# A new pair of heads every 8 hops of a two-way scan instead of every 13, and both chains of a pair in one tile

## The chip, the cores and the metric

The kernel runs on one core of one Trainium2 chip. The metric is the device time of one execution in microseconds (us). The core has five engines that the profile tells apart: PE (TensorE, the matrix products; its weight loads are listed as PEld), DVE (VectorE), ACT (ScalarE), POOL (GpSimd) and SP (SyncE, which here only issues DMAs). Each works through its own instructions in order and waits on semaphores for the others. Products are written to PSUM, everything else stands in SBUF, and large arrays in HBM.

## The reference

One layer of a model runs over 640 tokens: 512 latent tokens (group ii) and 128 context tokens (group i), with width 2048. After a wide input product, half of the channels go through a bidirectional delta-rule scan with 16 heads of 64 channels, the other half through a chunked gate (gMLP). Then come the output product, a SwiGLU block and the norms. The change touches the scan and what runs beside it:

```python
def _delta_scan(r, w, k, v, aa, bb, s0, reverse):
    def step(S, inp):
        r_t, w_t, k_t, v_t, a_t, b_t = inp
        sa = jnp.einsum('bhvk,bhk->bhv', S, a_t)
        S = S * w_t[:, :, None, :] + sa[..., None] * b_t[:, :, None, :] + v_t[..., None] * k_t[:, :, None, :]
        return S, jnp.einsum('bhvk,bhk->bhv', S, r_t)
    s_fin, ys = lax.scan(step, s0, xs, reverse=reverse)

def _rwkv7_bidir(p, s0, lp):
    ...
    for d in range(2):                      # forward, backward
        ...
        y, s_fin = _delta_scan(rh, decay, kd, vh, -kk, kk * heads(a), s0[:, d].astype(F32), reverse=(d == 1))
        out = out + _group_norm(y, lp['gn_w'], lp['gn_b']) + jnp.sum(rh * kd * lp['r_k'], axis=-1, keepdims=True) * vh
    o = (out.reshape(B, T, D_A) * gate).astype(dtype)

x = x + g1 * (jnp.concatenate([o_a, o_b], axis=-1) @ lp['w_out'])
```

The context scan starts from zero and its final states are an output; the latent scan starts from given states.

## The kernel before

The scan is done in chunks of 64 tokens: 8 chunks of the latents and 2 of the context. An earlier stage has written for each chunk and pair of heads a record to HBM (d_S: the matrices that carry a state over the chunk and that make its outputs), 128 partitions with 2 directions of 576 values, 576 KB. Eight pairs of heads (NPAIR) are worked through by the generator `recur(p)`. A pair has two chains: the latents with 8 steps, and the context with 2. A step takes three hops. In the first, PE multiplies the state by the record (w, L1464) and DVE adds what the record holds (W, L1469); the outputs of the step before are made here too (y, L1430 and L1435), and ACT takes them out with their sums (Y, L1449). In the second, PE makes u (L1480), and DVE and ACT copy the halves back into the record (L1483, L1484). In the third, PE makes the state's update (s, L1501) and DVE adds it to the decayed state (SG L1498, SN L1507; L1505 for a first step). A hop is one round of the loop at L1630; each generator in work goes one `yield` ahead per hop. `recur` starts and ends with a turn of the states (swap, L1406).

Three more things run in the same hops. `finish(p)` normalises the finished pair (POOL, ACT, DVE), turns it (pO, L1577), multiplies by the gate (pG, L1587) and stores it to d_o. A mixer, m3, hands out the second half of the output product: wide products of 128x320 (L1332 to L1334), which need pieces of w_out (raw, split into hi and lo), turned inputs (pxT, L1614) and add to x1T (L1345). `load_next` asks for the next record each time an output has been taken; there are 8 record buffers (NREC). SP issues all these loads in the order of its own list. PE's order in this stage is the order in which the program states the products; the other engines' orders and the places of the pools in SBUF are set by the framework when the program is built. The last products of the stage before (the gMLP's psp, with its additions sp on DVE) reach into the first hops.

OFF = 13 says how many hops lie between the starts of two pairs, so the loop has 13 x 7 + 26 = 117 hops, with two pairs in work. The names `ws`, `u`, `y0`, `y1`, `g` are PSUM tags: two buffers for `ws` (w, s and swap), one for each of the others.

## Time and profile before

| | |
|---|---|
| Time, median of 3 runs | 3182.96 us (3179.46 to 3184.34) |
| The profiled execution: its time | 3181.58 us |
| Its span, from first to last instruction | 3179.8 us |
| PE busy over the span | 3060.3 us (96%) |
| DVE busy over the span | 2321.0 us (73%) |
| First swap of the first pair | 1020.8 us from the span's start |
| Last swap of the last pair | 1307.7 us |

The views used below are the page, which sums up the whole span; the windows, which give each engine's busy time in a stretch, with the granted clock of PE, the mean busy share of the 16 DMA engines and what they moved; the waits, which say who waited for whom (total us, times, longest); the groups of instructions by line (busy time, mean ns of one, idle time of the engine just before them); the DMA issues; and the timeline, where a row is a start, a length, the engine, the line, output and inputs, and in brackets the engine's idle time before it and who ended it. A float32 product shows as two records there. Numbers such as 64*64 are the part of PE's array that the product takes. The ends of products are modelled, so starts are what is compared.

### The profile page before, as it was taken

The numbers are of one execution on the slowest core, as the hardware profiler recorded it, in microseconds if no ns is written. First come the engines' busy times: TensorE is split into PE (matmuls) and PEld (weight loads), VectorE is DVE, ScalarE is ACT, GpSimd is POOL, SyncE is SP. The second block draws the span as 40 slices with busy tenths as digits, with TensorE's granted clock in tenths as the row PEclk, the third lists the DMA queues.
The fourth block names the chain that finished last, engine by engine and source line by source line (L and its number), as shares of the span: only waits on it lengthen the run. The fifth ranks groups of instructions, "written<-read, shape, count | busy, mean of one in ns | idle before, by whom it ended". The sixth has DMA issues, their size and how long they took to land. (4 is left out here: it accounts for less than half of the span.)

```text
span 3179.8 us, 73098 instructions
## 1 busy us (share of the span) xinstructions
PE 3060.3 (96%) x28572; PEld 2860.0 (90%) x28572; DVE 2321.0 (73%) x4103; ACT 1449.0 (46%) x3173; POOL 1296.1 (41%) x1154
## 2 busy tenths in 40 slices
PE   7999999999998999999899999999999999999996
PEld 4788888888877777889899999999999999999996
DVE  4557686776756677677887787787877877877787
ACT  4244555555543443346444444444444444444365
POOL 1001222322321143320566566665666645554543
PEclk9999999999999999999999999999999999999998
DMA  9768988899886877455333443434334354554453
GB/s 342 241 187 240 237 236 213 214 233 235 223 228 190 251 240 246 134 153 174 105 119 118 127 123 107 124 116 126 120 108 130 107 183 146 163 163 141 115 174 122
DMA packets 742331, 552.97 MB, mean 174 GB/s; under 512 B 142112, under 2 KB 678720, under 8 KB 733152
## 3 DMA queue, kind: packets, MB, share of 16 engines
q1 hardware_dynamic: 727280, 529.73, 56.2%
q0 software_dynamic: 12288, 17.95, 2.4%
q8 instruction: 225, 3.69, 0.5%
q14 instruction: 122, 1.00, 0.1%
q10 hardware_dynamic: 2416, 0.60, 0.1%
HBM read 438.74 MB, written 111.69 MB: 173 GB/s over the span
## 5 line engine op out<-in xcount | busy, mean ns | idle before, releaser
L1932 PE MATMUL P<-xo,lo 128*128 128x320 f32 x2352 | 728.0, 310 | 7.5 <-DVE lo L1720 7.5
L1930 PE MATMUL P<-xo,hi 128*128 128x320 f32 x2352 | 728.1, 310 | 2.2 <-ACT hi L1719 2.2
L1931 PE MATMUL P<-xo,hi 128*128 128x320 f32 x2352 | 727.7, 309 | 0.0
L1720 DVE TENSOR_TENSOR lo<-raw,hi 128x512 fp32r<-128x512 f32 x532 | 506.0, 958 | 177.2 <-ACT hi L1719 175.4
L1719 ACT CAST hi<-raw 128x512 fp32r<-128x512 f32 x532 | 330.4, 622 | 505.5 <-PE P L1931 431.9
L1932 PEld LDWEIGHTS P<-xo,lo 128*128 128x128 f32 x2352 | 442.2, 188 | 8.0 <-DVE lo L1720 8.0
L1930 PEld LDWEIGHTS P<-xo,hi 128*128 128x128 f32 x2352 | 442.4, 188 | 2.4 <-ACT hi L1719 2.4
L1931 PEld LDWEIGHTS P<-xo,hi 128*128 128x128 f32 x2352 | 442.4, 188 | 0.0
L1830 POOL TENSOR_TENSOR raw<-raw 128x512 f32<-128x512 f32 x252 | 413.7, 1645 | 16.5 <-DVE lo L1720 3.3
L1930 PE MATMUL P<-xd,hi 128*128 128x320 f32 x1232 | 384.2, 312 | 8.5 <-ACT hi L1719 4.1
L106 PE MATMUL big<-h_hi,hi 128*128 128x320 f32 x1184 | 388.8, 328 | 0.7 <-DVE early L600 0.7
L1932 PE MATMUL P<-xd,lo 128*128 128x320 f32 x1232 | 384.3, 312 | 4.3 <-DVE lo L1720 4.0
L1931 PE MATMUL P<-xd,hi 128*128 128x320 f32 x1232 | 383.1, 311 | 0.0
L106 PE MATMUL big<-h_hi,lo 128*128 128x320 f32 x1184 | 365.5, 309 | 0.4 <-DVE lo L106 0.4
L106 PE MATMUL big<-h_lo,hi 128*128 128x320 f32 x1184 | 365.5, 309 | 0.0
L1830 POOL TENSOR_TENSOR t<-raw 128x512 f32<-128x512 f32 x84 | 134.8, 1605 | 460.6 <-DMA raw<-in_w_ffn_up_dram 399.2
L1719 ACT CAST hi<-rawd 128x512 fp32r<-128x512 f32 (+1 forms) x288 | 166.1, 586 | 230.0 <-PE P L1931 150.5
L106 PEld LDWEIGHTS big<-h_hi,hi 128*128 128x128 f32 x1184 | 223.7, 189 | 34.4 <-issue 29.0
L1720 DVE TENSOR_TENSOR lo<-rawd,hi 128x512 fp32r<-128x512 f32 (+1 forms) x288 | 217.5, 762 | 44.9 <-ACT hi L1719 41.5
L1930 PEld LDWEIGHTS P<-xd,hi 128*128 128x128 f32 x1232 | 233.4, 189 | 12.0 <-ACT P L2228 6.5
L1932 PEld LDWEIGHTS P<-xd,lo 128*128 128x128 f32 x1232 | 233.5, 190 | 7.1 <-DVE lo L1720 7.1
L1931 PEld LDWEIGHTS P<-xd,hi 128*128 128x128 f32 x1232 | 233.4, 189 | 0.0
(406 smaller groups left out, 6347.4 us busy)
## 6 DMA issues: line engine op xcount, KB each, us to landing
wt<-in_w_mod_dram SPq DMA_DIRECT2D x96, 1024.0 KB
raw<-in_w_ffn_gate_dram SPq DMA_DIRECT2D x182, 256.0 KB
raw<-in_w_ffn_up_dram SPq DMA_DIRECT2D x182, 256.0 KB
rec<-d_S SPq DMA_DIRECT2D x80, 576.0 KB
raw<-in_w_in_dram SPq DMA_DIRECT2D x166, 256.0 KB
rawd<-in_w_ffn_down_dram SPq DMA_DIRECT2D x128, 256.0 KB
raw<-in_w_out_dram SPq DMA_DIRECT2D x96, 256.0 KB
xd<-d_os SPq DMA_DIRECT2D x66, 320.0 KB
```

Source lines behind the costliest of these rows:

```text
L106: self.eng, self.run = eng, lambda: fn(*args, **kw)
L1719: S.copy(hi[:, 0:nk], raw[:, 0:nk])
L1720: V.tensor_sub(lo[:, 0:nk], raw[:, 0:nk], hi[:, 0:nk].bitcast(F32))
L1830: G.tensor_tensor(out=o[:, 0:nk], in0=p[:, 0:nk], in1=q[:, 0:nk], op=ALU.subtract)
L1930: TE.matmul(ps, hi[:, k, :], xk[:, 0, :], start=f, stop=False)
L1931: TE.matmul(ps, hi[:, k, :], xk[:, 1, :], start=False, stop=False)
L1932: TE.matmul(ps, lo[:, k, :], xk[:, 0, :], start=False, stop=l)
```

## The change

The distance of two pairs becomes 8 hops, so that three are in work in most hops, and the loop has 8 x 7 + 26 = 82. In a hop the pair in its second stage (u) now stands first, then the one in its first (w and y), then the one in its third (s). Both chains of a pair share one PSUM tile in each stage, and the products of both are stated before the first copy or addition. The tiles that a pair holds longer get more buffers: Y and ys five instead of three, ST/SN ten instead of seven, bv and g2r two instead of one. At the end of the loop the sixth pair is not finished yet, so its o block is loaded when it is.

```diff
 ROWO = 4
 RAWB = 13
 WTAIL = -12
-OFF = 13
+OFF = 8
 MB = 6
 KCOST = 35.0
 GORD = (0, 1, 1, 2, 2, 3, 3, 8)
...
             for d in range(2):
                 for h in range(2):
                     TE.matmul(ps[hsl(h), d, :], src[hsl(h), d, :], I2[hsl(h), :], start=True, stop=True)
-            o = sm.tile([P, 2, CH], F32, tag="ST", name="ST", bufs=7)
+            o = sm.tile([P, 2, CH], F32, tag="ST", name="ST", bufs=10)
             V.tensor_copy(o, ps)
             return o
 
         def recur(p):
 
             u = U[p]
-            u.Y = rw.tile([P, 2, NCH, CH], F32, tag=f"Y{p % 3}", name="Y")
-            u.ys = sm.tile([P, 2, NCH], F32, tag=f"ys{p % 3}", name="ys", bufs=1)
+            u.Y = rw.tile([P, 2, NCH, CH], F32, tag=f"Y{p % 5}", name="Y")
+            u.ys = sm.tile([P, 2, NCH], F32, tag=f"ys{p % 5}", name="ys", bufs=1)
             chains = [[False, swap(u.s0)], [True, None]]
             if p + 2 < NPAIR:
                 load_s0(p + 2)
...
 
             for step in range(len(LATC)):
                 act = [c for c in chains if step < len(seqs[c[0]])]
-                Ws = []
-                for ctx_, ST in act:
+                Ws = [None] * len(act)
+                if any(ST is not None for _, ST in act):
+                    ws = pws.tile([P, 2, 2, CH], F32, tag="ws", name="w_ps")
+                for e, (ctx_, ST) in enumerate(act):
                     r = recs[p, ctx_, step]
-                    if ST is None:
-                        Ws.append(None)
-                        continue
-                    w_ps = pws.tile([P, 2, CH], F32, tag="ws", name="w_ps")
-                    for d in range(2):
+                    if ST is not None:
+                        for d in range(2):
+                            for h in range(2):
+                                TE.matmul(ws[osl(h), e, d, :], r[hsl(h), d, F_R:F_R + CH], ST[hsl(h), d, :],
+                                          start=True, stop=True)
+                for e, (ctx_, ST) in enumerate(act):
+                    r = recs[p, ctx_, step]
+                    if ST is not None:
+                        W = Ws[e] = sm.tile([P, 2, CH], F32, tag="W", name="W", bufs=4)
                         for h in range(2):
-                            TE.matmul(w_ps[osl(h), d, :], r[hsl(h), d, F_R:F_R + CH], ST[hsl(h), d, :],
-                                      start=True, stop=True)
-                    W = sm.tile([P, 2, CH], F32, tag="W", name="W", bufs=4)
-                    for h in range(2):
-                        q = osl(h)
-                        V.tensor_add(W[q], w_ps[q], r[q, :, F_Z + CH * h:F_Z + CH * h + CH])
-                    Ws.append(W)
+                            q = osl(h)
+                            V.tensor_add(W[q], ws[q, e], r[q, :, F_Z + CH * h:F_Z + CH * h + CH])
                 outputs()
                 yield 1
                 both = pu.tile([P, 2, 2, CH], F32, tag="u", name="u_ps")
                 for e, ((ctx_, ST), W) in enumerate(zip(act, Ws)):
                     r = recs[p, ctx_, step]
-                    ups = both[:, e]
                     for d in range(2):
                         for h in range(2):
                             q = osl(h)
-                            TE.matmul(ups[q, d, :], r[q, d, F_T:F_T + CH],
+                            TE.matmul(both[q, e, d, :], r[q, d, F_T:F_T + CH],
                                       r[q, d, F_Z + CH * h:F_Z + CH * h + CH] if W is None else W[q, d, :],
                                       start=True, stop=True)
-                    V.tensor_copy(r[0:64, :, F_Z + CH:F_Z + P], ups[0:64])
-                    S.copy(r[64:128, :, F_Z:F_Z + CH], ups[64:128])
+                for e, (ctx_, ST) in enumerate(act):
+                    r = recs[p, ctx_, step]
+                    V.tensor_copy(r[0:64, :, F_Z + CH:F_Z + P], both[0:64, e])
+                    S.copy(r[64:128, :, F_Z:F_Z + CH], both[64:128, e])
                 yield 1
-                for ch in act:
+                ss, made = pws.tile([P, 2, 2, CH], F32, tag="ws", name="s_ps"), []
+                for e, ch in enumerate(act):
                     ctx_, ST = ch
                     cc = seqs[ctx_][step]
                     r = recs.pop((p, ctx_, step))
                     late.append((cc, r, ST))
                     if step + 1 == len(seqs[ctx_]) and not ctx_:
                         continue
-                    s_ps = pws.tile([P, 2, CH], F32, tag="ws", name="s_ps")
-                    SN = sm.tile([P, 2, CH], F32, tag="ST", name="SN", bufs=7)
                     ge = gend[:, p].rearrange("p d c -> p (d c)")[:, flip(cc)].unsqueeze(2)
+                    SG = None
                     if ST is not None:
                         SG = sm.tile([P, 2, CH], F32, tag="SG", name="SG", bufs=4)
                         V.tensor_tensor(out=SG, in0=ST, in1=ge.to_broadcast([P, 2, CH]), op=ALU.mult)
                     for d in range(2):
                         for h in range(2):
-                            TE.matmul(s_ps[hsl(h), d, :], r[:, d, F_X + CH * h:F_X + CH * h + CH],
+                            TE.matmul(ss[hsl(h), e, d, :], r[:, d, F_X + CH * h:F_X + CH * h + CH],
                                       r[:, d, F_Z + CH * h:F_Z + CH * h + CH], start=True, stop=True)
+                    made.append((e, ch, ge, SG))
+                for e, ch, ge, SG in made:
+                    SN = sm.tile([P, 2, CH], F32, tag="ST", name="SN", bufs=10)
                     for d in range(2):
-                        if ST is None:
-                            V.tensor_scalar_mul(SN[:, d, :], s_ps[:, d, :], ge[:, d])
+                        if SG is None:
+                            V.tensor_scalar_mul(SN[:, d, :], ss[:, e, d, :], ge[:, d])
                         else:
-                            V.scalar_tensor_tensor(out=SN[:, d, :], in0=s_ps[:, d, :], scalar=ge[:, d], in1=SG[:, d, :],
+                            V.scalar_tensor_tensor(out=SN[:, d, :], in0=ss[:, e, d, :], scalar=ge[:, d], in1=SG[:, d, :],
                                                    op0=ALU.mult, op1=ALU.add)
                     ch[1] = SN
                 yield 1
...
 
         def finish(p):
 
-            bv = rw.tile([P, T], F32, tag="bv", name="bv")
+            bv = rw.tile([P, T], F32, tag="bv", name="bv", bufs=2)
             nc.sync.dma_start(bv, d_bv[p])
-            g2r = sm.tile([P, 2, P], F32, tag="g2r", name="g2r", bufs=1)
+            g2r = sm.tile([P, 2, P], F32, tag="g2r", name="g2r", bufs=2)
             nc.sync.dma_start(g2r[:, 0, :], g2[0, 0:P, p * P:(p + 1) * P])
             for k in range(4):
                 nc.sync.dma_start(g2r[32 * k:32 * k + 32, 1, :], g2[0, P:160, p * P:(p + 1) * P])
...
         act, ends, nxt, gate = [], [], 0, gates()
         hops = OFF * (NPAIR - 1) + 26
         for hop in range(hops):
-            for gen in list(ends):
-                if next(gen, 0) == 0:
-                    ends.remove(gen)
+            for x in list(ends):
+                if next(x[1], 0) == 0:
+                    ends.remove(x)
             if hop >= 10:
                 next(gate, None)
             if hop == OFF * nxt and nxt < NPAIR:
                 act.append((nxt, recur(nxt)))
                 nxt += 1
-            for p, gen in sorted(act, key=lambda x: (hop - OFF * x[0]) % 3 == 0):
+            for p, gen in sorted(act, key=lambda x: 2 - (hop - OFF * x[0]) % 3):
                 if next(gen, None) is None:
                     act.remove((p, gen))
-                    ends.append(finish(p))
+                    ends.append((p, finish(p)))
             m3.run(m3.left / (hops - hop - WTAIL))
         assert not act
-        for kb in range(7):
+        for kb in range(ends[0][0]):
             o_load(kb)
         while ends:
-            for gen in list(ends):
-                if next(gen, 0) == 0:
-                    ends.remove(gen)
+            for x in list(ends):
+                if next(x[1], 0) == 0:
+                    ends.remove(x)
+                    o_load(x[0])
             m3.run(1.2)
-        o_load(7)
         m3.drain()
```

The order of the instructions on the engines moves at three places that matter here. The first is PE's order where a pair has two chains in its second stage, shown with the semaphores that an instruction waits for (DVE_49 and Activation_49 count what DVE and ACT have done, DMAHW a DMA). Before, in the first step of the fourth pair (u_ps<-W is the latent chain, u_ps<-rec the context's first step):

```order
L1480 MATMUL u_ps<-W,rec 64x64 [waits DVE_49,Activation_49]
L1480 MATMUL u_ps<-W,rec 64x64 [waits DVE_49]
L1480 MATMUL u_ps<-W,rec 64x64 x2
L1480 MATMUL u_ps<-rec 64x64 [waits DMAHW2_49,Activation_49]
L1480 MATMUL u_ps<-rec 64x64 x3
L1501 MATMUL s_ps<-rec 64x64 x4
```

And the same pair (the fourth) in the changed kernel:

```order
L1480 MATMUL u_ps<-W,rec 64x64 [waits DVE_49,Activation_49]
L1480 MATMUL u_ps<-W,rec 64x64 [waits DVE_49]
L1480 MATMUL u_ps<-W,rec 64x64 x2
L1480 MATMUL u_ps<-rec 64x64 [waits DMAHW6_49]
L1480 MATMUL u_ps<-rec 64x64 x3
L1463 MATMUL w_ps<-SN,rec 64x64 [waits DMAHW0_49,DVE_49]
L1463 MATMUL w_ps<-SN,rec 64x64
L1463 MATMUL w_ps<-SN,rec 64x64 [waits DVE_49]
```

The second chain's first product no longer waits for ACT, and the w products of another pair follow where s stood.

The second place is PE at the start of the scan, as a difference (the names are those above; I is the unit matrix, s the given states):

```order
-L1614 MATMUL pxT<-ident,x1T 128x128
+L1619 MATMUL pxT<-ident,x1T 128x128
+L106 MATMUL psp<-wspT,vt_13853 128x128 x5
 L1406 MATMUL swap<-I_68,s_13979 64x64 x4
 L1332 MATMUL big<-oh,hi 128x320
```

The gMLP's last products now stand ahead of the first swap; before, they stood behind the first u product, with the swap, the first w products and 12 wide ones ahead of them.

The third is SP at the same time, with the waits. Before:

```order
L1395 DMA rec<-d_S 128x2x576 [waits DMAHW2_49]
L1400 DMA s_13979<-in_state_rwkv_dram 128x2x64 [waits DMAHW3_49]
L1400 DMA s_13981<-in_state_rwkv_dram 128x2x64 [waits DMAHW4_49]
L1395 DMA rec<-d_S 128x2x576 [waits DMAHW5_49]
L1395 DMA rec<-d_S 128x2x576 [waits DMAHW6_49]
L1395 DMA rec<-d_S 128x2x576 [waits DMAHW7_49]
```

And in the changed kernel:

```order
L1395 DMA rec<-d_S 128x2x576 [waits DMAHW6_49]
L1609 DMA x1T<-in_x_sample_dram 128x4x128 [waits DMAHW7_49,PE_49]
L1609 DMA x1T<-in_x_prompt_dram 128x128 [waits DMAHW0_49]
L415 DMA raw<-in_w_out_dram 128x4x128 [waits DMAHW1_49,DVE_49]
L415 DMA raw<-in_w_out_dram 128x4x128 [waits DMAHW2_49,DVE_49,Activation_49]
L415 DMA raw<-in_w_out_dram 128x4x128 [waits DMAHW3_49,DVE_49]
L1523 DMA bv<-d_bv 128x640 [waits DMAHW4_49]
L1523 DMA bv<-d_bv 128x640 [waits DMAHW5_49]
L1400 DMA s_13979<-in_state_rwkv_dram 128x2x64 [waits DMASW4_49,DMASW3_49,DMASW5_49,DMASW2_49,DMASW6_49,DMASW1_49,DMASW7_49,DMASW0_49,DMAHW6_49,DVE_49,Pool_49]
```

The first pair's states were loaded after four records and waited for an earlier DMA alone. Now they are loaded behind all eight records, an input block, three pieces of w_out and two bv, and the load also waits for DVE, POOL and POOL's DMAs (DMASW): its tile lies where the gMLP's tiles were, and what it waits for on DVE is the last sp addition.

## The prediction, made before the changed kernel was run

> **What bounds the kernel now.** I read the page's head first, then the windows around the scan, then who waited for whom there, then the timelines of single hops.
>
> ```profile
> span 3179.8 us, 73098 instructions
> PE 3060.3 (96%) x28572; PEld 2860.0 (90%) x28572; DVE 2321.0 (73%) x4103; ACT 1449.0 (46%) x3173; POOL 1296.1 (41%) x1154
> ...
> 1020.00:1320.00 300.00, 276.29 (x4253) 232.01 (x4251) 214.46 (x665) 115.66 (x511) 102.84 (x128) 0.98 0.71 221
> ```
>
> TensorE (PE) bounds the whole program, and the scan too: from 1020 to 1320 us it is busy 276.3 of 300 us. Only this stretch changes, so all that can be won lies in two places: the 23.7 us in which PE idles there, and what inside its busy time is not arithmetic. The waits inside the stretch:
>
> ```profile
> PE u_ps L1480 <- ACT rec L1484: 14.6, 17, 1.3
> PE psp L106 <- DVE vt L106: 3.8, 1, 3.8
> PE pO L1577 <- ACT x1T L1615: 1.2, 2, 0.8
> ...
> PE s_ps L1501 <- ACT rec L1484: 1.1, 2, 0.8
> ```
>
> One wait holds most of it: the u product waits for ScalarE (ACT) 17 times, 14.6 us. Another 3.8 us is one wait of the last gMLP product (psp), which stands among the first hops. The remaining 5 us is scattered.
>
> **The u wait goes: 14.6 us.** One case in the timeline, PE, then VectorE (DVE) and ACT:
>
> ```profile
> 1038.45 0.45 PE L1480 MATMUL u_ps<-W,rec 64*64 64x64 f32 x8
> 1039.59 0.45 PE L1480 MATMUL u_ps<-W,rec 64*64 64x64 f32 x8 [0.69 <-ACT rec L1484]
> ...
> 1038.95 0.28 DVE L1483 COPY rec<-u_ps 64x128 f32<-64x128 f32 x1
> ...
> 1039.28 0.26 ACT L1484 COPY rec<-u_ps 64x128 f32<-64x128 f32 x1
> ```
>
> The first chain's products end at 1038.9, DVE copies them, ACT copies the other half after DVE (both write the same record), and only then may PE write the second chain into the same tile. That happens where two chains are in work: steps 0 and 1 of 8 pairs, 16 times, which is the 17 of the row but one. Now all products stand ahead of the copies, and the second chain's first product no longer waits for ACT in the order shown. What is late next is the copy of the first chain, by the 0.4 us of the second chain's products; its reader, the s product, is one hop away, so that costs nothing. If that cover were gone it would be 16 times 0.4, 6 us. I take the whole 14.6.
>
> **Fewer hops, fewer changes of tile shape: 12 us.** The loop has 13 x 7 + 26 = 117 hops before and 8 x 7 + 26 = 82 after, with the same products in them. The cost of a change between the 64-row products and the wide ones is inside PE's busy time:
>
> ```profile
> 1101.37 0.31 PE L1334 MATMUL big<-oh,lo 128*128 128x320 f32 x1
> 1101.61 0.27 PE L1480 MATMUL u_ps<-W,rec 64*64 64x64 f32 x2
> ...
> 1101.89 0.40 PE L1430 MATMUL y_ps<-SN,rec 64*64 64x64 f32 x8
> 1102.22 0.69 PE L1435 MATMUL y_ps<-rec 128*64 128x64 f32 x16
> 1102.83 0.45 PE L1430 MATMUL y_ps<-SN,rec 64*64 64x64 f32 x8
> 1103.21 0.42 PE L1332 MATMUL big<-oh,hi 128*128 128x320 f32 x1
> 1103.47 0.31 PE L1333 MATMUL big<-ol,hi 128*128 128x320 f32 x1
> 1103.62 0.31 PE L1334 MATMUL big<-oh,lo 128*128 128x320 f32 x1
> ```
>
> Wide products start 0.15 us apart (1103.47 to 1103.62). From wide to small it is 0.24 (1101.37 to 1101.61), 0.09 more. Small ones go at some 0.03 each; the 8 from 1102.83 take 0.38 until the wide one, 0.14 more, and that one takes 0.26 instead of 0.15: 0.25 in all. Between the two small shapes (8 in 0.33, 16 in 0.61) it is some 0.1. Counted along PE's order from the first swap to the last gate product, the changes fall from 353 to 275: 34 fewer into small, 34 fewer into wide, 10 fewer among the small. That is 34 x 0.09 + 34 x 0.25 + 10 x 0.1 = 12.6; I take 12. Its bounds: nothing, if the drains hid other waits, and 12.6.
>
> **The start gets later: -6.9 us.** Here the order speaks against the change. psp now stands ahead of the first swap, and the load of the first states stands behind eight records, three weight pieces and two bv on SyncE's queue (SP) and now waits for the last gMLP addition on DVE (sp<-psp): the larger pool puts the state's tile where that stage still works.
>
> ```profile
> 1020.79 0.45 PE L1406 MATMUL swap<-I,s 64*64 64x64 f32 x8
> 1024.13 0.33 PE L1480 MATMUL u_ps<-W,rec 64*64 64x64 f32 x2
> 1028.25 1.71 PE L106 MATMUL psp<-wspT,vt 128*128 128x128 f32 x10 [3.79 <-DVE vt L106]
> ...
> 1029.57 0.89 DVE L106 TENSOR_TENSOR sp<-psp,bsp 128x512 f32<-128x512 f32 x2 [0.32 <-PE psp L106]
> ...
> 1001.62 1.06 SPq L1400 DMA_DIRECT2D s<-in_state_rwkv_dram  x2
> ...
> d_o<-praw POOLq DMA_DIRECT2D x1, 320.0 KB, 2.5
> ...
> bsp<-in_b_spatial_dram POOLq DMA_DIRECT2D x1, 64.0 KB, 5.0
> ```
>
> Before, the states were asked for at 1001.6 and PE swapped them at 1020.8. After, PE reaches psp at 1020.8 and waits until its input is ready, 1028.2 as before: 7.4 us idle. psp ends at 1029.8, the two additions at 1030.5, then SP issues the load. How long 64 KB take then, no row of before says; the nearest are 2.5 us (320 KB, later, at a quiet time) and 5.0 (64 KB, behind the records). By then nothing else is on the queues, so I take 2.5: the swap starts at 1033.1, 3.3 us after psp, and 5.8 with the other end. Idle time at the start is 10.7 against 3.8: 6.9 lost (9.4 at the other end).
>
> ```profile
> 1000.00:1020.00 20.00, 17.17 (x125) 16.82 (x121) 13.10 (x23) 8.54 (x17) 3.15 (x5) 0.78 0.87 291
> 1020.00:1040.00 20.00, 14.85 (x154) 12.29 (x152) 15.30 (x38) 6.07 (x19) 1.78 (x2) 0.83 0.48 139
> ...
> 1031.87 0.63 PE L1332 MATMUL big<-oh,hi 128*128 128x320 f32 x1
> 1032.83 0.47 PE L1332 MATMUL big<-oh,hi 128*128 128x320 f32 x1
> ```
>
> After a wait PE is slow for a while: the granted clock is 0.83 of full over 1020 to 1040, and three wide products take 0.96 us at 1031.9 where they take 0.44 otherwise. From 1028.25 to about 1035.8 some 7.5 us went at half pace, 3.8 us lost. The same comes after the new wait, so it is in neither sum. [...]
>
> **The end: 1.3 us won.**
>
> ```profile
> 1307.69 0.45 PE L1406 MATMUL swap<-I,SN 64*64 64x64 f32 x8
> ...
> 1321.34 0.80 PE L1577 MATMUL pO<-I,Y 64*64 64x64 f32 x20 [1.28 <-POOL Y L1550]
> ```
>
> After the last swap PE has 78 wide products (11.5 us) until the last pair's turned output, which comes 13.6 us after the swap; 1.28 us are idle. After the change 81 wide products, the sixth pair's 20 turns and 8 gate products stand there, some 14 to 15 us: covered. The wide products that move from the hops to the end are the same number in all.
>
> **What the denser hops may cost: 8 us.** Three things have no row in the trace of before. First, the records: eight buffers as before, but a record needed 8 places later comes after 6.4 hops on average instead of 10.4, and three hops of each are its use. Its load then has 3 hops or more, some 10 us, where it had 6 or more, some 15.
>
> ```profile
> SPq L1395 <- PE y_ps L1435: 97.0, 48, 4.5
> SPq L415 <- DVE lo L417: 28.7, 8, 8.6
> ```
>
> SP mostly waits for the release itself (97.0 us), so loads leave at once; 576 KB at the 221 GB/s of the window row are 2.7 us; no wait of PE names a record's DMA. I take 1 us (0 to 12). Second, DVE. It is busy 214.5 us of the window; the scan's own part is
>
> ```profile
> L1469 DVE TENSOR_TENSOR W<-w_ps,rec 64x128 f32<-64x128 f32 x144 | 41.6, 289 | 13.7 <-PE w_ps L1464 9.8
> ...
> L1507 DVE SCALAR_TENSOR_TENSOR SN<-s_ps,gend,SG 128x64 f32<-128x64 f32 x128 | 29.9, 276 | 7.7 <-PE s_ps L1501 5.9
> ...
> L1483 DVE COPY rec<-u_ps 64x128 f32<-64x128 f32 x80 | 22.3, 279 | 15.4 <-PE u_ps L1480 7.9 <-PE w_ps L1464 5.0 <-issue 1.3
> ...
> L1498 DVE TENSOR_TENSOR SG<-SN,gend 128x128 f32<-128x128 f32 x56 | 17.9, 333 | 0.5
> ```
>
> 41.6 + 29.9 + 22.3 + 17.9 = 111.7 us over 8 x 26 = 208 pair-hops, 0.54 each. With three pairs that is 1.6 us a hop, and the other 102.8 us over 82 hops 1.25: 2.9 us, in a hop that PE needs about 3.2 for (287 us from first to last swap less 24 idle and 12 of changes, over 82 hops, and a little more with three pairs). 90% on an engine that works in order, where the same sum before gave some 80%. I take 5 us (0 to 18). Third, at the start the ACT and DVE orders now hold the cast of the gate weights and of an o block, whose loads come late, ahead of copies of the scan: 2 us (0 to 5).
>
> **The sum.** 14.6 + 12 - 6.9 + 1.3 - 8 = 13.0 us. The profiled execution took 3181.58 us for its span of 3179.8; the median of the runs is 1.4 above it. 3181.6 - 13 = 3168.6, and I write 3169 for the median too.
>
> **Rivals.** (a) *Records come late and the scan is slower than before.* Eight buffers serve 10 records per 8 hops, so a buffer's round is 6.4 hops; 3.25 of them are use, and the load may take 3.15 hops, 10 us at 3.2 a hop. If it takes L, the hop is L / 3.15. It decides against the change from 13 us / 48 steady hops = 0.27 a hop on, 3.47, that is L = 10.9. A weight load that blocks SP for the 8.6 us of the row above, plus 2.7, is 11.3 to 12: hop 3.8, 48 x 0.6 = 29 us lost, 3198. For it: SP issues in order, and the traffic per hop grows. Against: such blocks are 8 in 300 us.
> (b) *DVE takes what PE is given.* If DVE's queue holds the s to w step up in each of the 48 steady hops by 0.2 us beyond what I took, 10 us go: 3179, no change to speak of. For it: the 90% above. Against: today w and s wait for DVE in next to no row. [...]
> (c) *The change of shape is hidden today* and fewer of them save nothing: 13 - 12 = 1 us, 3180.6. Against: the 0.24 and 0.26 stand in the starts of products that wait for nothing.
>
> **How the numbers follow.** Forecast 0.62, (a) 0.10, (b) 0.18, (c) 0.10. The forecast's own range is from 3159 (no new wait, 21 + 2) to 3176. About 0.2%, 6.4 us, is what a measurement of this kernel tells from no change: the forecast is faster nearly always (0.60), (b) and (c) in a part (0.08), (a) is slower, and a part of (b): faster 0.68, same 0.20, slower 0.12. The range for 8 in 10 takes in (b) and (c) and the start of (a): 3155 to 3187.
>
> **What would show it.** In the changed profile: u_ps <- ACT rec falls from 14.6 to under 2; psp waits some 7 us and the first swap starts near 1033 behind the load of s; the last swap ends near 1289 instead of 1308 (13 won plus the work moved behind it); DVE is busy some 80% of the stage. A PE wait on the records' DMA, or waits of w_ps and s_ps on DVE of more than 15 us together, would make the prediction wrong; so would a start later than 1036.

## The result

| | before | after |
|---|---|---|
| Time, median | 3181.21 us (3178.16 to 3184.34, 4 runs) | 3153.39 us (3150.58 to 3161.06, 4 runs) |
| Ratio after / before | | 0.9916 [0.9895, 0.9938] |
| The profiled execution: time, span | 3181.58, 3179.8 us | 3155.66, 3153.8 us |
| First swap, last swap (start of its last record) | 1020.8, 1307.9 us | 1029.2, 1270.7 us |

Faster, by 28 us where 13 were forecast, and just below the range. The profile after, its waits of PE from 1015 to 1300 us:

```profile
PE psp L106 <- ACT gq L106: 7.3, 1, 7.3
PE swap L1406 <- DMA s<-in_state_rwkv_dram: 2.7, 1, 2.7
PE u_ps L1480 <- ACT rec L1486: 1.9, 3, 0.8
PE s_ps L1503 <- ACT rec L1486: 1.8, 1, 1.8
PE s_ps L1503 <- DVE ST L1408: 1.8, 5, 0.4
```

The u wait fell from 14.6 us to 1.9, the psp wait rose from 3.8 to 7.3, and the swap now waits for its load. No wait for a record's DMA appears, and none for DVE over 2 us. The timeline at the start (PE, with SP's load of the states), then the two u chains of one step:

```profile
1013.53 0.71 PE L106 MATMUL pvt<-ident,praw 128*128 128x128 f32 x5
1024.00 2.48 PE L106 MATMUL psp<-wspT,vt 128*128 128x128 f32 x10 [7.31 <-ACT gq L106]
1027.05 0.90 SPq L1400 DMA_DIRECT2D s<-in_state_rwkv_dram  x2
1029.19 0.69 PE L1406 MATMUL swap<-I,s 64*64 64x64 f32 x8 [2.71 <-DMA s<-in_state_rwkv_dram]
...
1041.93 0.68 PE L1480 MATMUL u_ps<-W,rec 64*64 64x64 f32 x16
1042.54 0.41 PE L1332 MATMUL big<-oh,hi 128*128 128x320 f32 x1
```

The 16 records of u run without the gap that stood between the chains. The windows from the first to the last swap, of before and then of after (length, then busy time of PE, its weight loads, DVE, ACT and POOL, the granted clock, the DMA share and GB/s):

```profile
1020.79:1307.92 287.13, 263.42 (x4169) 219.89 (x4168) 205.45 (x645) 111.06 (x500) 91.70 (x114) 0.98 0.72 225
```

```profile
1029.19:1270.66 241.47, 233.61 (x4079) 203.77 (x4080) 192.40 (x622) 109.39 (x492) 89.49 (x112) 0.99 0.82 259
```

The stretch is 45.7 us shorter: 15.8 us less idle time of PE (23.7 to 7.9) and 29.8 us less busy time. Part of that is work moved out of the stretch, and it starts later, so a fixed measure is needed. Below, **the stage** is the time from the last pvt product of the gMLP (the x5 row at 1013.53, whose last product starts at 1013.96; 1018.13 before) to the first product C of the SwiGLU block:

```profile
1464.09 0.41 PE L1853 MATMUL C<-xo,hi 128*128 128x320 f32 x1 [0.58 <-DVE rs L1741]
```

```profile
1434.64 0.41 PE L1858 MATMUL C<-xo,hi 128*128 128x320 f32 x1 [0.58 <-DVE rs L1746]
```

That is 446.0 us before and 420.7 after, 25.3 less. What stands ahead of it and behind it is the same program; it differs by a few us between executions (C to the end is 1713.6 to 1721.1 us in the profiles below). Two profiles of one kernel differ by up to 2.6 us in the stage. For the changed kernel that difference is one stretch in which the granted clock stood at 0.50, behind the scan (1383.46 to 1390.29 in the first profile, none there in the second). Stages are read from one profiled execution each, and ratios from all executions, so the two need not agree to the microsecond.

### The profile page after: what moved, and what is told of

Same layout as the page of the kernel before. It is cut to its first block, busy times and chain, and to the rows that moved or that the text cites. A ratio compares the mean times of both kernels' runs of the same rounds, so it can differ in the third digit from the quotient of the medians.

```text
span 3153.8 us, 73060 instructions
## 1 busy us (share of the span) xinstructions
PE 3041.3 (96%) x28572; PEld 2854.0 (90%) x28572; DVE 2311.1 (73%) x4103; ACT 1451.9 (46%) x3173; POOL 1302.1 (41%) x1154
## 5 line engine op out<-in xcount | busy, mean ns | idle before, releaser
L1935 PEld LDWEIGHTS P<-xd,hi 128*128 128x128 f32 x1232 | 234.0, 190 | 10.4 <-ACT hi L1724 5.4
```

What stands on the lines that cost most here:

```text
L1935: TE.matmul(ps, hi[:, k, :], xk[:, 0, :], start=f, stop=False)
```

## The experiments

All runs in one table. "u" says whether both chains' u products stand ahead of the copies, "w, s" whether both chains share a tile there. PE idle is the length of the window from first to last swap less PE's busy time in it.

| Kernel | distance | u | w, s | stage us | swap to swap us | PE idle us | ratio to before |
|---|---|---|---|---|---|---|---|
| before | 13 | old | old | 446.0 | 287.1 | 23.7 | 1 |
| u alone | 13 | new | old | 429.5 | 270.6 | 11.9 | 0.9963 [0.9948, 0.9978] |
| tiles alone | 13 | new | new | 425.1 | 267.4 | 11.1 | 0.9929 [0.9912, 0.9946] |
| pairs alone | 8 | old | old | 448.7 | 271.5 | 28.2 | 1.0003 [0.9993, 1.0014] |
| u back | 8 | old | new | 435.5 | 259.4 | 22.0 | 0.9990 [0.9977, 1.0003] |
| after | 8 | new | new | 420.7 | 241.5 | 7.9 | 0.9916 [0.9895, 0.9938] |
| after again | 8 | new | new | 418.1 | 241.6 | 8.4 | 0.9921 [0.9906, 0.9936] |
| wide split | 8 | new | new | 428.4 | 253.0 | 4.8 | 0.9940 [0.9922, 0.9959] |
| DVE more | 8 | new | new | 424.0 | 246.4 | 10.9 | 0.9950 [0.9934, 0.9966] |
| six records | 8 | new | new | 450.5 | 272.2 | 26.6 | 1.0012 [0.9998, 1.0026] |
| s0 early | 8 | new | new | 415.7 | 252.0 | 15.3 | 0.9908 [0.9890, 0.9926] |
| s0 early again | 8 | new | new | 417.8 | 253.0 | 16.5 | 0.9903 [0.9876, 0.9930] |
| 18 us ahead | 8 | new | new | 414.6 | 238.3 | 11.0 | 0.9901 [0.9875, 0.9927] |
| 24 us ahead | 8 | new | new | 408.7 | 230.1 | 10.0 | 0.9893 [0.9862, 0.9924] |

### Each half of the change alone

**The pairs alone** have the distance, loop and buffers of the change, and the stages of before:

```diff
-OFF = 13
+OFF = 8
...
-            o = sm.tile([P, 2, CH], F32, tag="ST", name="ST", bufs=7)
+            o = sm.tile([P, 2, CH], F32, tag="ST", name="ST", bufs=10)
```

> Three pairs in work and 82 hops, but each chain with its own products, copies and tiles as in the kernel before. PE's order and its 266 changes of tile shape between first and last swap are those of the changed kernel. Theory A (the two parts add up: the u wait is worth its idle time, the hops their changes of shape, and the small products go quicker in the denser hops): the u wait stays near 14 us, the busy time from first to last swap falls to about 234 us as in the changed kernel, and the kernel takes about 14 us more than the changed one, 3167. Rival B (the extra 9 us of busy time, beyond the 21 forecast, come from the u waits, behind which PE's clock drops): busy time from swap to swap stays near 242 and the kernel takes 20 to 23 us more than the changed one, about 3175.

Measured: 3178.08 us, ratio 1.0003, nothing won. The stage is 2.7 us longer. PE's waits from 1015 to 1300 us:

```profile
PE u_ps L1480 <- ACT rec L1484: 17.1, 16, 1.9
PE psp L106 <- ACT gq L106: 7.3, 1, 7.3
PE s_ps L1501 <- DVE W L1469: 6.9, 18, 1.5
```

The u wait grew a little, and a new one came: with a tile per chain, s must wait until DVE has read a w tile (W) out of one of the two `ws` buffers, which three pairs go through faster (0.4 us in 2 before). PE's busy time from swap to swap is 243.3 us, near the 242 of rival B and not the 234 of theory A.

**The tiles alone** keep distance 13 and the buffers of before, and take the stages of the change (L1455 to L1515):

```diff
-OFF = 8
+OFF = 13
...
-            for p, gen in sorted(act, key=lambda x: 2 - (hop - OFF * x[0]) % 3):
+            for p, gen in sorted(act, key=lambda x: (hop - OFF * x[0]) % 3 == 0):
```

> 13 hops between pairs and two pairs in work as before; only the shared tiles and the products ahead of the copies are taken over. PE's order, its 348 changes of shape between first and last swap and the early load of the states are those of the kernel before. Theory A: the u wait of 14.6 us falls to under 2, busy time from first to last swap stays at about 263 us, the kernel gains 14 us: 3167. Rival B: the granted clock stays at 1.00 from 1040 us on and busy time falls by 6 to 9 us as well; gain 20 to 23 us, about 3160. A third possibility, that the time given back goes into waits for DVE, would show less than 8 us.

Measured: 3154.97 us, ratio 0.9929, as forecast by B: the stage is 20.8 us shorter. So nearly the whole gain is there without the three pairs, and more than the idle time of the u wait. From first to last swap:

```profile
1017.36:1284.76 267.40, 256.32 (x4169) 215.93 (x4168) 201.81 (x645) 110.67 (x500) 91.24 (x114) 0.99 0.77 242
```

### Where in the tiles the gain lies

**u alone**: the kernel before, only the copies of u moved behind the second chain's products.

```diff
-                    V.tensor_copy(r[0:64, :, F_Z + CH:F_Z + P], ups[0:64])
-                    S.copy(r[64:128, :, F_Z:F_Z + CH], ups[64:128])
+                for e, (ctx_, ST) in enumerate(act):
+                    r = recs[p, ctx_, step]
+                    V.tensor_copy(r[0:64, :, F_Z + CH:F_Z + P], both[0:64, e])
+                    S.copy(r[64:128, :, F_Z:F_Z + CH], both[64:128, e])
```

> The kernel before with one edit: in the second stage both chains' u products stand ahead of the copies. Distance 13, buffers, w and s tiles as before. A (a wait costs what PE idles in it): the u wait falls from 14.6 us to under 2, PE's busy time between the first and the last swap stays at 263, 14 to 15 us faster than before. B (PE is slow for a while after such waits, so they cost more than they last): 20 to 24 us faster, busy time down by 5 to 8, no stretch of the scan after 1040 us with a granted clock under 0.97: that is, all that the shared tiles without the new distance gave. C (the shared w and s tiles gave the rest): 14 to 15 us faster as in A, and the 7 us of busy time that the shared tiles won are not there.

**u back**: the changed kernel with that part undone.

```diff
-                for e, (ctx_, ST) in enumerate(act):
-                    r = recs[p, ctx_, step]
```

(The two copies thereby stand in the loop of the products again.)

> The changed kernel with one edit: in the second stage the first chain's copies stand ahead of the second chain's products again. Distance 8, shared w and s tiles as in the change. A: 16 waits of 0.9 to 1.1 us come back, 15 to 17 us slower than the changed kernel. B: 20 to 25 us slower, granted clock under 0.95 in several stretches of the scan, the time of the pairs alone (ratio 1.000). If the distance itself covers the waits (another pair's products between them): under 5 us slower.

**After again**, the changed kernel unedited, run beside these two:

> The changed kernel once more, beside the three variants below, so that differences of a few us are read on one chip. Nothing is edited. Ratio to the kernel before 0.990 to 0.993 (it was 0.9916 [0.9895, 0.9938]).

Measured: u alone 3164.67 us, ratio 0.9963, u back 3173.46, 0.9990, the changed kernel 3150.80, 0.9921. The stage of u alone is 16.5 us shorter than before's, between A and B. From first to last swap, of u alone:

```profile
1014.69:1285.29 270.60, 258.73 (x4168) 217.56 (x4168) 203.82 (x645) 111.31 (x500) 91.99 (x114) 0.99 0.77 239
```

Against before, 11.8 us are idle time and 4.7 are busy time. By the ratio it is 12 us faster (7 to 17 by its interval): that agrees with A's 14 to 15 and excludes B's 20 to 24, and it can't tell 14.6 from 16.5. So the 4.7 us are a reading of the two profiles. PE's products and their order are the same in both, so the busy time fell because PE was slowed less: the windows of 20 us after 1040 have a granted clock of 0.94, 0.98 and 0.91 in three places before, by estimate (0.06 + 0.02 + 0.09) x 20 = 3.4 us lost, and 1.00 everywhere with u alone. They are two stretches at 0.50 (before; columns as above):

```profile
1097.42:1100.83 3.41, 3.41 (x46) 2.84 (x45) 2.02 (x9) 0.74 (x5) 0.00 (x0) 0.50 0.66 188
1165.69:1169.10 3.41, 3.41 (x46) 2.84 (x45) 2.36 (x9) 0.53 (x4) 0.00 (x0) 0.50 0.38 76
```

How that comes about is to be seen in u back, in PE's timeline behind one wait, and in two windows, the one with the wait and the next:

```profile
1066.38 0.38 PE L1480 MATMUL u_ps<-W,rec 64*64 64x64 f32 x4 [2.01 <-ACT rec L1484]
...
1068.66 0.47 PE L1334 MATMUL big<-oh,lo 128*128 128x320 f32 x1
1068.93 0.47 PE L1332 MATMUL big<-oh,hi 128*128 128x320 f32 x1
1069.20 0.47 PE L1333 MATMUL big<-ol,hi 128*128 128x320 f32 x1
1069.46 0.47 PE L1334 MATMUL big<-oh,lo 128*128 128x320 f32 x1
...
1069.98 0.31 PE L1333 MATMUL big<-ol,hi 128*128 128x320 f32 x1
1070.12 0.31 PE L1334 MATMUL big<-oh,lo 128*128 128x320 f32 x1
```

```profile
1063.11:1066.52 3.41, 1.40 (x20) 1.07 (x21) 2.67 (x8) 1.42 (x7) 0.00 (x0) 1.00 0.82 235
1066.52:1069.93 3.41, 3.41 (x39) 3.17 (x38) 1.24 (x4) 0.79 (x5) 0.00 (x0) 0.50 0.73 216
```

After a wait of 2.0 us wide products start 0.27 us apart instead of 0.15, until 1069.7. At distance 8 the u edit is worth 14.8 to 17.4 us of the stage (435.5 against 420.7 and 418.1), as A had it, and 0.0069 of the time, 22 us, as B had it. About 5 us of that difference lie outside the stage or in executions that were not profiled; they are not explained.

The shared tiles of w and s are the rest: at distance 13 they take 4.4 us off the stage (u alone against tiles alone), at distance 8 they take 13.2 (pairs alone against u back). The ratios say 11 us (0.9963 against 0.9929) and only 4 us (1.0003 against 0.9990, with intervals that overlap): the profiled execution of the pairs alone was the slowest of its ten, so the 13.2 is the profiles' figure and not shown by the times. At 13 the row of a step with two chains shows where: u alone, then tiles alone.

```profile
1051.54 1.00 PE L1503 MATMUL s_ps<-rec 128*64 128x64 f32 x16
1052.47 0.41 PE L1332 MATMUL big<-oh,hi 128*128 128x320 f32 x1
```

```profile
1053.83 0.80 PE L1503 MATMUL s_ps<-rec 128*64 128x64 f32 x16
1054.56 0.41 PE L1332 MATMUL big<-oh,hi 128*128 128x320 f32 x1
```

The same 16 records take 0.93 us until the next product, or 0.73. Over the sixteen steps with two chains the median is 0.93 against 0.57, and the sum 15.6 against 10.8 us: 4.8 us, about what the stage shows. Of a step's 0.36 us 0.14 are idle time and the rest counts as busy; neither stands in a row of waits. At 8 the named wait of s for W goes too: u back has no such row over 1 us, where the pairs alone had 6.9 us. So C was right on where 4 to 5 us lay; that the u wait costs more than it lasts, as B said, shows in the profiles with 4 to 5 us instead of the 5 to 8 that B gave.

### The terms of the denser loop

**Wide split**: the changed kernel hands out the mixer's products in two parts per hop, which puts 75 of the 78 saved changes of tile shape back (350 against 275 to the last gate product).

```diff
-            for p, gen in sorted(act, key=lambda x: 2 - (hop - OFF * x[0]) % 3):
+            share = m3.left / (hops - hop - WTAIL)
+            for n, (p, gen) in enumerate(sorted(act, key=lambda x: 2 - (hop - OFF * x[0]) % 3)):
+                if n == 2:
+                    m3.run(share / 2)
...
-            m3.run(m3.left / (hops - hop - WTAIL))
+            m3.run(share / 2 if len(act) > 2 else share)
```

> The changed kernel with the wide products of a hop handed out in two parts, one ahead of the last of the three pairs and one behind it: 341 changes of tile shape between first and last swap instead of 266, 42 more into small, 42 more into wide, 9 fewer among the small. Theory A (0.09, 0.25 and 0.1 us each): 42 x 0.34 - 0.9 = 13.4 us more than the changed kernel, 3167, in PE's busy time, with waits as they are. Rival C (the drains are hidden and fewer changes save nothing): within 3 us of the changed kernel.

```profile
1025.64:1278.66 253.02, 248.21 (x4082) 208.17 (x4083) 194.53 (x623) 108.82 (x495) 87.94 (x112) 0.99 0.78 247
```

PE's busy time from swap to swap is 248.2 instead of 233.6 us for the same products, 14.6 more where the price of the shape changes gave 13.4; idle time falls by 3.1. The stage is 7.8 to 10.4 us longer, the ratio 0.0019 to 0.0024 higher, 6 to 8 us (the intervals overlap). The price stands. Against the second profile of the changed kernel, which had the same time at half clock, the stage's 10.4 us are 14.6 of busy time less 4.2 of idle time: waits that the added products cover.

**DVE more**: 64 additions on DVE that nothing reads, ahead of the copies of u.

```diff
+                X = sm.tile([P, 2, CH], F32, tag="X", name="X", bufs=1)
+                V.tensor_add(X, r[:, :, F_R:F_R + CH], r[:, :, F_T:F_T + CH])
                 for e, (ctx_, ST) in enumerate(act):
```

> The changed kernel with one addition more on VectorE in each second stage, 128x128 values of a record into a tile that nothing reads, ahead of the copies of u: 64 of about 0.33 us, 21 us of VectorE in all. If VectorE has no margin in the denser hops (rival (b) of the prediction): 48 steady hops by 0.2 to 0.33 us, 10 to 16 us slower than the changed kernel. If it has margin (busy 15 to 19 of 20 us in the changed kernel, with no long wait of PE for it): under 4 us slower, with s and w waiting for VectorE under 8 us.

Its group, from 1020 to 1290 us (busy time, mean ns; idle time ahead of it and what ended it):

```profile
L1484 DVE TENSOR_TENSOR X<-rec 128x128 f32<-128x128 f32 x64 | 20.4, 319 | 13.0 <-DMA rec<-d_S 12.6
```

The dose was larger than planned: in DVE's order the additions stand early and also wait 12.6 us for records. Of these 33 us of DVE the stage shows 3.4 to 6.0 and the ratio 0.0029, 9 us. So DVE had most of that to spare. By the stage that is nearer to the expectation with margin, by the ratio (9 us, where the one without began at 10) nearer to the other; the profiled execution was the fastest of the four by 6 us, so how much margin there is stays open between 3 and 9 us of cost.

**Six records**: `NREC = 8` becomes 6 in the changed kernel.

> The changed kernel with six record buffers instead of eight; nothing else. Rival (a) put the margin of the records into question: a buffer's round is 6 / 10 of 8 hops, 4.8 hops, of which 3.25 are use, so a load has 1.55 hops, 4.6 us at the 2.95 us per hop of the changed kernel (241.5 us from first to last swap, 82 hops), against 9.3 us with eight buffers. If a load with its place in SyncE's queue takes 6 us, a hop becomes 3.9 us: some 48 x 0.9 = 43 us slower than the changed kernel, and PE waits for the records' DMA by name. If loads take 3 to 4 us: within 4 us of the changed kernel, and then eight buffers had 5 us to spare each.

```profile
PE w_ps L1463 <- DMA rec<-d_S: 19.8, 14, 2.4
```

```profile
1029.07:1301.30 272.23, 245.59 (x4080) 212.84 (x4080) 193.22 (x622) 109.68 (x492) 90.09 (x112) 0.95 0.76 234
```

All of the gain is gone, 0.0091 of the time, 29 us: 19.8 us of named waits, and 12 us more busy time at a clock of 0.95 instead of 0.99. 82 hops in 272.2 us are 3.32 a hop; if the loads set it, one takes by estimate 1.55 x 3.32 = 5.1 us with its place in the queue. Eight buffers allow, by the same estimate, 3.15 x 2.95 = 9.3 us. Rival (a) is a real mechanism, which begins between six and eight buffers.

### The start, and a faster version

**s0 early**: the given states in the pool `rw`, which does not lie where the gMLP still works.

```diff
-            U[p].s0 = sm.tile([P, 2, CH], F32, tag="s0", name="s0", bufs=2)
+            U[p].s0 = rw.tile([P, 2, CH], F32, tag="s0", name="s0", bufs=2)
```

> The changed kernel with the given states' two buffers in the pool of the records instead of the small tiles' pool; the load of the first states then stands after four records and waits for no gMLP addition, and the first swap stands ahead of the gMLP's last products again. Theory: the first swap starts within 1 us of the input turn ahead of it instead of 12.8 us after it, the wait for the gMLP's products stays at 4 to 6 us, and the kernel takes 5 to 7 us less than the changed one, about 3147. Rival: the scan's start is bound by the gMLP's chain on DVE anyway, whose end also holds up the first W: then the same time within 2 us.

```profile
1014.79 0.71 PE L106 MATMUL pvt<-ident,praw 128*128 128x128 f32 x5
1017.88 0.45 PE L1406 MATMUL swap<-I,s 64*64 64x64 f32 x8
1025.47 2.50 PE L106 MATMUL psp<-wspT,vt 128*128 128x128 f32 x10 [5.63 <-DVE vt L106]
1029.63 0.69 PE L1463 MATMUL w_ps<-ST,rec 64*64 64x64 f32 x8 [1.66 <-issue]
```

The swap stands 2.7 us behind the last pvt again instead of 15.2, but psp still waits 5.6 us behind it, and w follows late. Of the 10.0 us idle (7.3 + 2.7) 7.3 stay (5.6 + 1.7): 2.7 won. The stage agrees (416.8 in the mean of two against 419.4), and the ratio, 0.9908 and 0.9903 against 0.9916 and 0.9921, does not contradict it. So neither the 5 to 7 us expected nor the rival's 2 us was met.

**More products ahead of the scan**: on top of s0 early the mixer hands out 18 or 24 us of its products first.

```diff
-        m3.run(4.0 + 8.0)
+        m3.run(4.0 + 14.0)
```

> The changed kernel with the given states in the pool of Y and bv, so that their load does not wait for the gMLP (as in the run with s0 early), beside the next two on one chip. The first swap stands right behind the turns of the inputs again, the psp wait stays at 5.6 us. 3 to 6 us faster than the changed kernel; ratio 0.990 to 0.992.

> The kernel with s0 early and one edit: the mixer hands out 18 us of its products ahead of the scan instead of 12, so that 43 wide products instead of 22 stand between the last turn of the gMLP's values and its psp product. 21 x 0.147 = 3.1 us of the 5.6 us wait are covered. By its idle time alone: 3 us faster than with s0 early. If PE is slow for a while after a wait whatever its length: just that. If the shorter wait is also followed by less slow time (granted clock 0.74 in 1020 to 1040 before): 4 to 6 us.

> The same with 24 us: 55 wide products there, 33 x 0.147 = 4.9 us covered, the wait under 1 us. By idle time alone 5 us faster than with s0 early; with the slow stretch gone as well (0.26 x 20 = 5 us at a granted clock of 0.74) 8 to 10 us. Rival: the products handed out earlier wait for their pieces of w_out, which SyncE loads in turn: then the wait goes to those and nothing is won.

With 24 us (`4.0 + 20.0`), PE's waits from 1000 to 1300 us and the window 1020 to 1040:

```profile
PE big L1332 <- ACT hi L416: 3.0, 1, 3.0
PE u_ps L1480 <- ACT rec L1486: 2.6, 3, 1.2
PE s_ps L1503 <- DVE ST L1408: 1.8, 5, 0.4
PE y_ps L1435 <- issue: 1.1, 1, 1.1
PE psp L106 <- DVE vt L106: 1.0, 1, 1.0
```

```profile
1020.00:1040.00 20.00, 19.03 (x239) 16.48 (x239) 12.58 (x40) 6.73 (x22) 0.60 (x1) 1.00 0.85 247
```

The psp wait fell to 1.0 us and the clock of that window rose to 1.00 (0.74 with s0 early, 0.93 at 18 us), and the stage to 408.7 us, 8 below s0 early, as the expectation with the slow stretch gone had it. But a piece of w_out is now waited for (hi, 3.0 us), and the medians of the three kernels, run together, are equal, 3145.5 us each; the profiled execution of the last was its fastest, 3132.64, the others 3144.2 to 3147.3. So 24 us ahead is best in the profile and not shown to be better in time. All three lie at 0.989 to 0.990 of before.

## Why the prediction was wrong in size

The direction and the main mechanism were right. To see which terms of the sum were off, the stage can be split in three: PE's idle time; what was lost at half clock (an estimate: half of PE's busy time in the stretches with a granted clock of 0.50, where wide products start 0.27 us apart instead of 0.15); and the rest, busy time at full clock.

| Stage, us | length | idle | lost at half clock | rest |
|---|---|---|---|---|
| before | 446.0 | 31.2 | 8.2 | 406.5 |
| u alone | 429.5 | 19.4 | 3.8 | 406.3 |
| tiles alone | 425.1 | 18.5 | 1.7 | 404.9 |
| after | 420.7 | 25.0 | 7.3 | 388.3 |
| after again | 418.1 | 25.4 | 4.1 | 388.6 |
| wide split | 428.4 | 21.2 | 4.1 | 403.1 |

The sum, term by term, from these rows; where two values stand, they are of the two profiles of the changed kernel:

| Term | forecast | measured | from |
|---|---|---|---|
| the u wait | -14.6 | -16.5 (idle -11.8, half clock -4.4, rest -0.3) | u alone |
| shared tiles of w and s | 0 | -4.4 (half clock -2.1 of it) | tiles alone less u alone |
| fewer changes of shape | -12 | -15 | wide split: 14.6 for 75, here 78 |
| later start, PE idle | +6.9 | +6.2 | 7.3 + 2.7 less 3.8 |
| half clock, at the start and behind the scan | 0 | +5.6, +2.4 | after less tiles alone |
| the end, PE idle | -1.3 | -0.4 | idle from last swap to C, 7.5 and 7.1 |
| denser hops, PE idle | +8 | +0.6, +1.0 | 7.9, 8.3 from swap to swap less 11.1 - 3.8 of tiles alone |
| left over | | -1 | |
| sum | -13.0 | -25.3, -27.9 | the stage |

**"I take the whole 14.6"** came out near the 16.5 of the stage, in part by luck: two errors went opposite ways. Only 11.8 us of idle time went with the wait, since other waits grew. In u alone s waits 2.5 us for ACT, where it had 1.1, and w 1.1 us for SN, where it had none:

```profile
PE s_ps L1503 <- ACT rec L1486: 2.5, 4, 0.8
PE w_ps L1464 <- DVE SN L1509: 1.1, 2, 0.8
```

I had taken the later copies as free, and they are not quite. And 4.4 us of half clock went too, which I had not counted: I had read the slow stretch only after the long waits at the start ("so it is in neither sum"); the shorter waits in the scan had it too, 3.4 us in the windows before.

**The shared tiles of w and s have no term.** I priced one of three shared tiles, since the list of waits named only u. The stall at s stood in no row of waits, 0.36 us in a step with two chains. With three pairs the old tiles cost 13 us by the profiles and 4 by the ratios. No run has the new u and the old w and s at distance 8, so whether the denser loop would gain anything without the shared tiles is not shown; with all stages old it gains nothing (pairs alone).

**"What the denser hops may cost: 8 us"** is the step that failed most. The bounds of records, DVE and the start's orders began at zero, and I took values inside them, 1, 5 and 2 us, without a row for any. From swap to swap, less the psp wait, PE idles 7.9 and 8.3 us in the changed kernel and 7.3 in the tiles alone: the denser hops cost about 1 us, 7 less than forecast. Records have by estimate 9.3 us against some 5.1. DVE is busy 192.4 of 241.5 us, the 80% I named for the stage; the 90% in a hop was no bound, since 33 us more of DVE cost 3 to 9.

**"Fewer changes of tile shape: 12 us"** had the mechanism right and the size low: 15 us by the wide split, and the rest of the stage falls by 16 to 17 from the tiles alone to the changed kernel. In all, the three pairs take 4.4 to 7.0 us off the stage (after against tiles alone), because the later start and its half clock take most of that back. The ratios of these kernels, 0.9929 against 0.9916 and 0.9921, have intervals that overlap, so the gain of the three pairs is a reading of the profiles.

**The start** came as worked out: the swap 12.6 us later behind the last pvt, 12.3 forecast; psp waits 7.3 us; the load of s, issued at 1027.05, was there 2.1 us later (2.5 taken). The slow stretch was not the same, though: the clock stood at 0.50 from 1029.15 to 1035.98 before, with PE busy for 6.2 us, and from 1021.66 to 1035.31 after, with PE busy for 8.6, so by the same estimate 3.1 and 4.3 us were lost there. The 2 us that the low end of the range (21 + 2) adds are shown by no run: the slow stretch at the start cost 1.2 us more than before, not 2 less. The forecast of a last swap near 1289 failed with the sum: it came at 1270.7, 4 us of that because this execution reached the last pvt 4 us earlier.

**The rivals.** (a) did not happen with eight buffers; with six its named wait appears and the gain is gone. (b): no wait for DVE over 2 us in the rows after, and DVE more, where 33 us of DVE cost 3 to 9. (c): the changes of shape are paid in PE's busy time, 14.6 us for 75. The range missed because its low end took in a forecast without any new wait but no gain that the list of waits did not name.

## What to carry to other kernels

The length of a wait in the list is not what removing it brings. Other waits can take over a part (here 14.6 us were named and 11.8 of idle time won), and more can hang on it: look in the windows for a granted clock under 1.00 behind it (4.4 us here), and compare the starts of products for stalls that stand in no list. More work in flight helps only after the shared buffers no longer tie the chains together: here, by the profiles, three pairs were worth nothing with the old tiles and 4 to 7 us with the new. And before an upper bound is taken as a cost, ask for the margin in rows: one experiment with a smaller buffer count or an added operation tells it.

## What the runs showed of the hardware

In the profiles of before and after the granted clock changes in steps of 3.41 us: each stretch at 0.50 lasts one step or a multiple of it (3.41 us at 1097.42 before, 6.83 at 1029.15, 13.65 at 1021.66 after). In the rows here the half clock follows how much PE idles within one step, and not how long one wait is. In u back the 2.01 us wait lies in one step (1063.11 to 1066.52, above). With six records, behind a wait of 2.30 us, wide products again start 0.27 us apart:

```profile
1083.75 0.27 PE L1463 MATMUL w_ps<-SN,rec 64*64 64x64 f32 x2 [2.30 <-DMA rec<-d_S]
...
1086.31 0.47 PE L1334 MATMUL big<-oh,lo 128*128 128x320 f32 x1
1086.58 0.47 PE L1332 MATMUL big<-oh,hi 128*128 128x320 f32 x1
```

In the kernel before, PE idles for only 1.34 us in the step ahead of the stretch at 1097.42.

```profile
1094.01:1097.42 3.41, 2.07 (x31) 1.63 (x30) 3.41 (x10) 1.78 (x12) 0.00 (x0) 1.00 0.98 335
```

In the changed kernel a longer wait, 1.85 us, is divided between two steps, and neither is followed by the half clock:

```profile
1046.35 0.45 PE L1503 MATMUL s_ps<-rec 128*64 128x64 f32 x8 [1.85 <-ACT rec L1486]
```

```profile
1042.14:1045.55 3.41, 2.36 (x33) 1.96 (x29) 2.17 (x7) 0.61 (x3) 0.00 (x0) 1.00 0.66 212
1045.55:1048.96 3.41, 2.61 (x49) 2.21 (x49) 2.18 (x8) 0.99 (x3) 0.00 (x0) 1.00 0.95 331
```

Over the steps at full clock in the profiles of before and after, the half clock followed none in which PE idled for less than 1.27 us (1162.28 to 1165.69 before: 2.14 of 3.41 us busy), and the full clock none in which it idled for more than 1.55 us (1014.83 to 1018.24 after: 1.86 of 3.41 busy). Between the two both occur, and these runs do not show what decides there.
